# Chunk 1's first and last 16 rows stored partly by GpSimd's software queue (15 partitions) and partly by sync (113 partitions)

## The chip, the cores and the metric

The kernel runs on one core of a Trainium2 chip. The metric is the device time of one execution in microseconds (us). A run's time is given as the median of its executions; "span" is the length of the one execution that the profiler recorded, about 1.3 us shorter than its time. The data path matters most here: transfers between HBM (the chip's main memory) and SBUF (the core's 128-partition memory) run on 16 DMA engines, and the page of a profile counts the packets of all queues as shares of the same 16 (in the kernel before 97.5%, 0.6% and 0.4% for its three data queues). The traces do not number the engines; where this text speaks of one engine, its packets were chained, each starting within a few ns of where another ended.

## The reference

```python
x_flat = x.reshape(-1, 256)             # 32768 rows of 256 float32, 33.5 MB
y = x_flat @ W                          # W is 256 x 256
lora_out = ((x_flat @ lora_A) * lora_E) @ lora_B
return (y + scale * lora_out).reshape(16, 2048, 256)   # float32, 33.5 MB
```

The kernel folds the low-rank part into `W` first and then does one product per row. It reads 33.5 MB and writes 33.5 MB.

## The kernel before

The rows are cut into 4 chunks. In a chunk each of the 128 partitions holds 64 neighbouring rows (64 KB) in a buffer, a "home"; results are written over the inputs and stored from there. Sync issues nearly all transfers, in a fixed order: `L` is a load, `S` a store, followed by chunk, first row and last row.

```python
ORDER = [
    ("A",),
    # ... loads of chunks 0, 1 and of rows 0 to 16 of chunk 2 ...
    ("L", 2, 16, 64),
    ("S", 0, 0, 40),
    ("S", 0, 40, 64),
    ("L", 3, 0, 32),      # these two wait for the stores of chunk 0: three homes, four chunks
    ("L", 3, 32, 64),
    ("S", 1, 2, 64),
    ("S", 2, 0, 64),
    ("S", 3, 0, 64),
]
SHARED = (1, 0, 2)            # rows 0 and 1 of chunk 1 are stored apart:
SHARES = ((0, 5), (5, 126))   # partitions 0-4 and 5-125 by GpSimd, 126-127 by sync
HELD = (2, 16)                # where GpSimd issues them and then waits for ("S", 0, 0, 40)
# ...
            else:                                     # a store, in the sync program
                if c == SHARED[0]:
                    sync.wait_ge(s_shared, 1)
                    share(sync, SHARES[-1][1], P, stored_rest)
                sync.wait_ge(s_done, ends.index((c * ROWS + e) // CG - 1) + 1)
                sync.dma_start(out=y_chunks[c, :, s:e, :], in_=at_home).then_inc(...)
# ...
            if (c, b) == HELD:                        # in the GpSimd program
                gpsimd.wait_ge(s_shared, 1)
                for s, e in SHARES:
                    share(gpsimd, s, e, shared_stored)
                for op in HOLDERS:
                    gpsimd.wait_ge(stored[op], 16)
```

The odd split of two rows is there for its side effect: in the trace of the kernel before the 121-partition software store did not load all 16 DMA engines alike: 15 took four 4,096-byte packets each and one a single packet of 2,052 bytes, so one engine is spared 14 KB.

## Time and profile before

| | before |
|---|---|
| median of the first 3 runs | 162.38 us (161.68 to 162.63) |
| span of the profiled run | 160.4 us |
| moved | 67.43 MB, mean 420 GB/s |
| last store issued | 117.8 us |
| last packets of the 16 DMA engines end | 158.4 to 159.9 us, mean 158.9 |

From the page of the kernel before, the span, the busiest compute engine, and the DMA rows (40 slices of the span; DMA is the busy share of the 16 engines in tenths, where 9 is 90% or more):

```profile
span 160.4 us, 2030 instructions
PE 93.2 (58%) x782; PEld 82.0 (51%) x782; DVE 45.4 (28%) x66; ACT 66.1 (41%) x65; POOL 67.9 (42%) x72
DMA  7999999999899997989999999979998998998992
GB/s 259 444 409 460 441 415 482 425 400 466 376 523 454 405 392 317 482 351 421 472 411 460 417 409 482 511 333 459 491 433 360 507 441 360 507 425 376 507 425 114
q1 hardware_dynamic: 2308, 66.87, 97.5%
q0 software_dynamic: 112, 0.26, 0.4%
```

The DMA engines are full throughout and no compute engine is above 58%. The last two lines give a queue's packets, MB and share of the engines' time: the software queue (q0, GpSimd) carries 0.26 of 67 MB.

The timeline of sync's queue in the kernel before (start, duration, operation, count), its later part:

```profile
75.60 7.74 SPq L153 DMA_DIRECT2D home<-in_x_dram  x2
83.38 0.34 SPq L166 DMA_DIRECT2D out_dram<-home  x1
83.77 34.37 SPq L161 DMA_DIRECT2D out_dram<-home  x3
```

The last load is issued at 83 us, the store of chunk 1 at 83.8 us, and the last store at 117.8 us. From there to the end, 42 us, the queue only drains, so a compute engine or an issue that comes a few us later costs nothing.

The same kernel by stretches of the span (from:to, length, busy time and count of the engines, then TensorE's granted clock, the DMA share and GB/s):

```profile
core 0: us, PE busy (x) PEld busy (x) DVE busy (x) ACT busy (x) POOL busy (x), PEclk, DMA share, GB/s
66.00:74.00 8.00, 0.00 (x0) 0.00 (x0) 0.00 (x0) 0.00 (x0) 0.00 (x0) 0.50 1.00 432
74.00:82.00 8.00, 5.18 (x32) 4.52 (x33) 1.59 (x3) 1.65 (x2) 4.28 (x5) 0.61 1.08 463
100.00:106.00 6.00, 6.00 (x57) 5.56 (x56) 3.39 (x5) 4.76 (x5) 4.75 (x5) 1.00 1.12 480
106.00:118.00 12.00, 10.70 (x98) 9.70 (x96) 4.91 (x8) 9.11 (x9) 5.65 (x6) 1.00 1.03 444
118.00:150.00 32.00, 0.00 (x0) 0.00 (x0) 0.00 (x0) 0.00 (x0) 0.00 (x0) 0.55 1.00 434
```

The last two columns are the ones to read together. The share lies about 1 (its scatter of a tenth comes from packets at the edges of a stretch), and with it go about 434 GB/s. A 65,536-byte packet takes 2.418 us, 27.1 GB/s, and 16 engines at that rate make 434. So in this trace full engines go with full speed.

### The profile page before, as it was taken

What the parts mean: (1) busy time and instruction counts of PE and PEld (TensorE: products, weight loads), DVE (VectorE), ACT (ScalarE), POOL (GpSimd) and SP (SyncE); (2) the same over time, 40 slices, a digit from 0 to 9 for tenths busy, and PEclk for the clock granted to TensorE, in tenths of its full rate; (3) what the DMA queues carried; (4) which work ended last, traced back from release to release, by engine and by line L of the source; (5) the groups of instructions that cost most, each with busy time, mean ns of one, the idle gap of its engine ahead of it and who ended that gap; (6) DMA issues with size and microseconds to landing.
All of it is one profiled execution on the core that took longest, in us unless ns stands there. A gap on an engine that the chain in (4) does not pass through costs nothing.

```text
span 160.4 us, 2030 instructions
## 1 busy us (share of the span) xinstructions
PE 93.2 (58%) x782; PEld 82.0 (51%) x782; DVE 45.4 (28%) x66; ACT 66.1 (41%) x65; POOL 67.9 (42%) x72
## 2 busy tenths in 40 slices
PE   2979969959999990000899999999910000000000
PEld 1359958959999990000799999999900000000000
DVE  0155534525555550000155555555400000000000
ACT  3016774747777772000167777777720000000000
POOL 1527838377777731101677777777100000000000
PEclk9999999999999998555599999999996555555555
DMA  7999999999899997989999999979998998998992
GB/s 259 444 409 460 441 415 482 425 400 466 376 523 454 405 392 317 482 351 421 472 411 460 417 409 482 511 333 459 491 433 360 507 441 360 507 425 376 507 425 114
DMA packets 2631, 67.43 MB, mean 420 GB/s; under 512 B 496, under 2 KB 512, under 8 KB 708
## 3 DMA queue, kind: packets, MB, share of 16 engines
q1 hardware_dynamic: 2308, 66.87, 97.5%
q10 hardware_dynamic: 208, 0.28, 0.6%
q0 software_dynamic: 112, 0.26, 0.4%
q14 instruction: 3, 0.02, 0.0%
HBM read 33.85 MB, written 33.55 MB: 420 GB/s over the span
## 4 chain that ended last, share of the span: by engine, by line
DMA 43%; PE 26%; POOL 1%; ACT 1%; SPq 1%; issue 0%; ACTq 0%
DMA out_dram<-home 30%; PE psum_y L255 17%; DMA home<-in_x_dram 13%; PE psum_xt L244 9%; POOL stage L193 1%; ACT home L209 1%; SPq L153 0%; ACTq L213 0%; SPq L326 0%; SPq L290 0%
## 5 line engine op out<-in xcount | busy, mean ns | idle before, releaser
L209 ACT COPY home<-psum_y 128x1024 f32<-128x1024 f32 x64 | 64.8, 1012 | 49.6 <-PE psum_y L255 49.6
L193 POOL CAST stage<-home 128x1024 bf16<-128x1024 f32 x64 | 66.0, 1040 | 37.3 <-PE psum_xt L244 13.4
L255 PE MATMUL psum_y<-weff,xt 128*128 128x256 bf16 x512 | 67.3, 275 | 0.0
L228 DVE COPY xt<-psum_xt 128x1024 bf16<-128x1024 bf16 x64 | 44.3, 692 | 62.0 <-PE psum_xt L244 62.0
L255 PEld LDWEIGHTS psum_y<-weff,xt 128*128 128x128 bf16 x512 | 50.6, 99 | 5.5
L244 PE MATMUL psum_xt<-ident,stage 128*128 128x128 f32 x260 | 40.8, 281 | 20.6 <-POOL stage L193 20.1
L244 PEld LDWEIGHTS psum_xt<-ident,stage 128*128 128x128 f32 x260 | 31.2, 144 | 23.4 <-issue 22.1
L268 PE MATMUL psum_y<-ident 128*128 128x512 f32 x4 | 3.8, 1098 | 2.9 <-POOL ident L171 2.9
L166 POOL DMA_DIRECT2D out_dram<-home x2 | 1.2, 596 | 5.7 <-DMA home<-in_x_dram 5.7
L268 PEld LDWEIGHTS psum_y<-ident 128*128 128x128 f32 x4 | 1.2, 323 | 3.9 <-POOL ident L171 2.9
L218 DVE TENSOR_SCALAR ate<-psum_y,e_sb 16x256 f32<-16x256 f32 x1 | 0.5, 471 | 7.2 <-PE psum_y L271 7.2
L209 ACT ACT_TABLE_LOAD x1 | 1.3, 1283 | 2.0 <-SPq L290 2.0
L277 PE MATMUL psum_y<-b_sb,ate 16*128 16x256 f32 x4 | 1.3, 447 | 0.0
L277 PEld LDWEIGHTS psum_y<-b_sb,ate 16*128 16x128 f32 x4 | 0.8, 242 | 0.4 <-issue 0.3
L169 POOL MEMSET ident<- 128x128 f32 x1 | 0.2, 205 | 1.7 <-SPq L290 1.7
L271 PEld LDWEIGHTS psum_y<-ident,a_sb 128*16 128x16 f32 x2 | 0.3, 133 | 1.2 <-issue 1.2
L232 DVE TENSOR_TENSOR weff<-w_sb,psum_y 128x512 bf16<-128x512 f32 x1 | 0.7, 686 | 0.6 <-PE psum_y L277 0.6
L271 PE MATMUL psum_y<-ident,a_sb 128*16 128x128 f32 x2 | 0.6, 418 | 0.0
L171 POOL TENSOR_SCALAR_AFFINE_SELECT ident<-ident 128x128 f32<-128x128 f32 x1 | 0.3, 287 | 0.2 <-POOL ident L169 0.2
L312 POOL MEMSET const-float32-0.0<- 128x1 f32 x1 | 0.1, 98 | 0.2 <-issue 0.2
L312 POOL MEMSET const-bfloat16-1.0<- 128x1 bf16 x1 | 0.1, 101 | 0.0
L312 POOL MEMSET const-uint8-127<- 128x1 uint8 x1 | 0.1, 101 | 0.0
(1 smaller groups left out, 0.1 us busy)
## 6 DMA issues: line engine op xcount, KB each, us to landing
home<-in_x_dram SPq DMA_DIRECT2D x4, 4096.0 KB, 24.4
out_dram<-home SPq DMA_DIRECT2D x1, 7936.0 KB
home<-in_x_dram SPq DMA_DIRECT2D x3, 2048.0 KB, 13.2
home<-in_x_dram SPq DMA_DIRECT2D x1, 6144.0 KB, 58.2
out_dram<-home SPq DMA_DIRECT2D x1, 5120.0 KB, 48.7
home<-in_x_dram SPq DMA_DIRECT2D x1, 3072.0 KB, 20.0
out_dram<-home SPq DMA_DIRECT2D x1, 3072.0 KB, 46.4
home<-in_x_dram SPq DMA_DIRECT2D x1, 1024.0 KB, 5.5
```

The lines of the kernel that those rows point to most:

```text
L166: engine.dma_start(out=y_chunks[c, first:last, s:e, :], in_=home(c)[first:last, s:e, :]).then_inc(landed, 16)
L193: gpsimd.tensor_copy(out=stage[g % NS][:], in_=home(c)[:, b:b + CG, :]).then_inc(s_stage[g % UNROLL], 1)
L209: scalar.copy(out=home(c)[:, b:b + CG, :], in_=psum_y[g % NY][:]).then_inc(s_free[(g + NY) % UNROLL], 1)
L218: vector.tensor_scalar(out=ate[:], in0=psum_y[0][:R, :KT, :P], scalar1=e_sb[:], scalar2=float(scale), op0=ALU.mult, op1=ALU.mult,).then_in ...
L228: vector.tensor_copy(out=xt[g % NX][:], in_=psum_xt[g % NT][:].bitcast(BF16)).then_inc(s_xt[g % UNROLL], 1)
L232: vector.tensor_add(out=weff[:], in0=w_sb[:], in1=psum_y[1][:, :KT, :]).then_inc(s_free[0], 1)
L244: ins = tensor.transpose(psum_xt[i % NT][:, b, :], words[:, b, :], ident[:])
L255: ins = tensor.matmul(psum_y[i % NY][:, b, :], xt[i % NX][:, b, t::KT], weff[:, t, :], start=(t == 0), stop=(t == KT - 1),)
L268: tensor.matmul(psum_y[1][:, :2, :], ident[:], ident[:, None, :].to_broadcast([P, 4, P]), start=True, stop=True)
L271: ins = tensor.transpose(psum_y[0][:R, t, :P], a_sb[:, t, :], ident[:])
L277: ins = tensor.matmul(psum_y[1][:, t, :], ate[:, t, :], b_sb[:], start=True, stop=True)
L312: nc = _bacc.Bacc("TRN2", target_bir_lowering=False, num_devices=1)
```

## The change

Its intent is to spare one DMA engine more work than before: 32 KB in place of 14. Two tiny stores around the large software store are meant to choose the engine. The diff, cut to its core:

```diff
-    ("S", 1, 2, 64),
+    ("S", 1, 16, 48),
-SHARED = (1, 0, 2)
-SHARES = ((0, 5), (5, 126))
+SHARED = 1
+END_ROWS = 16
 # sync
-                if c == SHARED[0]:
+                if c == SHARED:
                     sync.wait_ge(s_shared, 1)
-                    share(sync, SHARES[-1][1], P, stored_rest)
+                    share(sync, end_rows(slice(16, P)), stored_rest)
+                    for q in (0, 3):
+                        share(sync, lambda rows: in_pieces(rows)[:1, q, :, :], stored_rest)
+                    sync.wait_ge(shared_stored, 3 * 16)
 # ...
+    def in_pieces(rows):
+        return rows[:].rearrange("p (q b) k -> p q b k", b=END_ROWS)
+    def end_rows(p):
+        return lambda rows: in_pieces(rows)[p, ::3, :, :]          # rows 0-15 and 48-63
+    def middles(p):
+        return lambda rows: in_pieces(rows)[p, 1:3, 0, :64]        # tiny, stored again later
 # GpSimd, at HELD
-                for s, e in SHARES:
-                    share(gpsimd, s, e, shared_stored)
+                for part in (middles(slice(0, 5)), end_rows(slice(1, 16)), middles(slice(5, 17))):
+                    share(gpsimd, part, shared_stored)
```

So the end rows, 32 KB per partition and 4 MB in all, now go as 112 partitions by sync, partition 0 by sync, and partitions 1 to 15 by GpSimd. The wait on `shared_stored` keeps the tiny stores from racing with the store of the middle rows.

More of the change, by code (lines that the diff above doesn't have):

```diff
@@ L103 @@
     stored_rest = nc.alloc_semaphore("stored_rest")
-    n_rest = 1 + sum(op[0] == "S" and op not in waited for op in ORDER)
+    n_rest = 3 + sum(op[0] == "S" and op not in waited for op in ORDER)
     ends = sorted((c * ROWS + e) // CG - 1 for kind, c, s, e in (op for op in ORDER if op[0] == "S"))
@@ L156, in sync_program, with share @@
             else:
-                if c == SHARED[0]:
+                if c == SHARED:
                     sync.wait_ge(s_shared, 1)
-                    share(sync, SHARES[-1][1], P, stored_rest)
+                    share(sync, end_rows(slice(16, P)), stored_rest)
+                    for q in (0, 3):
+                        share(sync, lambda rows: in_pieces(rows)[:1, q, :, :], stored_rest)
+                    sync.wait_ge(shared_stored, 3 * 16)
                 sync.wait_ge(s_done, ends.index((c * ROWS + e) // CG - 1) + 1)
                 sync.dma_start(out=y_chunks[c, :, s:e, :], in_=at_home).then_inc(stored.get(op, stored_rest), 16)
-        sync.wait_ge(shared_stored, 16 * len(SHARES))
-    def share(engine, first, last, landed):
-        c, s, e = SHARED
-        engine.dma_start(out=y_chunks[c, first:last, s:e, :], in_=home(c)[first:last, s:e, :]).then_inc(landed, 16)
+    def in_pieces(rows):
[4 more added lines that the diff above has]
+        return lambda rows: in_pieces(rows)[p, 1:3, 0, :64]
+    def share(engine, part, landed):
+        engine.dma_start(out=part(y_chunks[SHARED]), in_=part(home(SHARED))).then_inc(landed, 16)
     def gpsimd_program():
@@ L209, in scalar_program @@
             scalar.copy(out=home(c)[:, b:b + CG, :], in_=psum_y[g % NY][:]).then_inc(s_free[(g + NY) % UNROLL], 1)
-            if (c, b) == SHARED[:2]:
+            if (c, b + CG) == (SHARED, ROWS):
                 scalar.drain().then_inc(s_shared, 1)
```

## The prediction

> **What bounds the kernel now.** The DMA engines. The page gives 67.43 MB in a span of 160.4 us (420 GB/s); its DMA row stands at 7 to 9 tenths in nearly every slice, PE is 58% busy, POOL 42%, ACT 41%. The chain of waits ends with the last ScalarE copy at 116.73 us; the last store is issued at 117.8 us and 42 us of queued stores follow. So no compute wait moves the end. In the packet records a 65,536-byte packet takes 2.418 us (27.1 GB/s, 434 for 16 engines); 67.43 MB at that rate are 155.5 us. What is left to win is unevenness among the 16 engines.
>
> **How uneven.** I chained the packets of the trace, each starting where another ended, into 16 engines. Their last packets end from 158.42 to 159.89 us, mean 158.9. Perfect levelling is worth 1.0 us, 0.6%. The three last end at 159.37, 159.57 and 159.89. The one at 159.37 was some 1.2 us behind at 62 us, and is the one that the 121-partition software store already spares: 15 engines took four 4,096-byte packets each, this one a single 2,052-byte packet, 14 KB (0.5 us) less.[...] The other two were late for other causes: one shared with an 8,192-byte instruction fetch at 86.6 us (0.3 us gap and a packet 0.5 us long), one had eight 63,488-byte packets 0.15 us long each.
>
> **What the change does.** Chunk 1's end pieces (32 KB per partition) go as 112 partitions, 7 per engine, by sync (16,384-byte packets, 611 ns elsewhere in the trace), one partition spread over all, and 15 by the software queue, one per engine, so that one engine gets 32 KB less: 1.2 us instead of 0.5 us.[...] If it is the slow one, it ends near 158.8 us; all others get about 2 KB (0.07 us) more. The two other late engines then set the end: gain 0 to 0.4 us, perhaps 0.5 on average where runs spare differently.
>
> **Costs.** One more software store, about 0.6 us of GpSimd, inside a hold that already idles 10.8 us for a store of chunk 0. Sync now waits for the software stores (landed 7.7 and 12.5 us after issue before; I estimate 12 to 20 us, as more packets each wait behind a hardware packet of 1.5 us) before the middle of chunk 1: until 76 to 84 us. Before, that store was issued at 83.8 us with about 16 us of loads still queued. Both are off the path.
>
> **Prediction.** 161.9 us, range 161.0 to 163.3. Chances: faster 0.01, same 0.97, slower 0.02.
>
> **What would show it.** The DMA row stays full to the end; the 15-partition store has data on 15 engines; the spared engine is no longer among the last three; the sync wait leaves no hole.
>
> **What would make it wrong.** Another engine spared than the slow one: the slow one then ends about 0.5 us later. Or [...]16,384-byte packets take longer than 611 ns: 1 to 3 us slower.

Three passages that no trace or run of this case shows are cut from it, and marked: a comparison for the 121-partition store, how the tiny stores were to choose the engine and why each execution should then spare the same one, and how 16,384-byte packets might come to take longer. 161.9 us is the 162.38 us of the first three runs less about 0.5, the upper end of the gain named. That one partition would be spread over all engines no trace had shown; it is a forecast, and the result below contradicts it. The 1 to 3 us of the last sentence stand without a derivation, as the author's estimate.

## The result, and the profile after

| | before | after |
|---|---|---|
| median | 162.03 us (161.68 to 162.63, 4 runs) | 169.03 us (167.83 to 170.64, 4 runs) |
| span of the profiled run | 160.4 us | 167.7 us |
| last packets end | 158.4 to 159.9, mean 158.9 | 160.4 to 167.4, mean 163.3 |
| last store issued | 117.8 us | 122.5 us |

The ratio is 1.0403 (95% interval 1.0332 to 1.0474): slower, far outside the predicted range of 161.0 to 163.3. A ratio here is the mean time of one kernel's fast runs over that of the other's fast runs of the same rounds, so not quite the ratio of the medians. One of the four runs of after (170.64) counts as slow and is not in the ratio; the profiled one is fast.

The page of the changed kernel, the same lines as above:

```profile
span 167.7 us, 2033 instructions
PE 93.1 (56%) x782; PEld 81.8 (49%) x782; DVE 45.4 (27%) x66; ACT 66.1 (39%) x65; POOL 68.6 (41%) x73
DMA  7999999999999899998999999999999999999960
GB/s 274 406 434 459 404 469 453 414 430 403 418 547 399 375 344 469 389 285 365 422 426 424 430 430 352 385 395 391 465 430 485 438 406 422 485 406 422 438 281 16
q1 hardware_dynamic: 2548, 66.63, 94.5%
q0 software_dynamic: 112, 0.50, 1.8%
```

The DMA row is as full as before and the bytes are the same within 0.02 MB, yet the span is 7.3 us longer. The software queue moves twice its former bytes and takes 1.8% of the engines' time in place of 0.4%. The last two GB/s figures (281 and 16) are a tail in which few engines still work.

Sync's queue in the changed kernel:

```profile
79.74 7.51 SPq L153 DMA_DIRECT2D home<-in_x_dram  x2
87.30 1.10 SPq L176 DMA_DIRECT2D out_dram<-home  x3
88.51 34.30 SPq L164 DMA_DIRECT2D out_dram<-home  x3
```

The loads of chunk 3 are issued 4.1 us later, because they wait for the stores of chunk 0, which landed later. Otherwise the order and the pace are as before: between the end rows at 87.3 us and the middle at 88.5 us there is no long wait, so the new wait for the software stores costs nothing here.

The stretches of the changed kernel:

```profile
66.00:74.00 8.00, 0.00 (x0) 0.00 (x0) 0.00 (x0) 0.00 (x0) 0.00 (x0) 0.50 1.05 382
74.00:82.00 8.00, 1.04 (x5) 1.00 (x6) 0.00 (x0) 0.00 (x0) 2.02 (x2) 0.50 0.97 366
100.00:106.00 6.00, 6.00 (x57) 5.60 (x56) 3.04 (x5) 4.51 (x6) 4.81 (x5) 1.00 0.93 344
106.00:118.00 12.00, 12.00 (x112) 11.15 (x111) 6.31 (x10) 9.32 (x10) 9.37 (x9) 1.00 1.04 408
118.00:150.00 32.00, 3.37 (x31) 2.86 (x29) 1.30 (x2) 3.53 (x4) 0.00 (x0) 0.63 1.00 434
```

Here is the loss. The engines are busy (share 0.93 to 1.05), but at 66 to 82 us, when the software stores run, and at 100 to 118 us, when the end rows go out by sync, they move 344 to 408 GB/s. At 118 us all is well again. Busy engines with fewer bytes mean that single packets took longer.

The packet records show which. A 16,384-byte packet takes 611 ns elsewhere in these traces. Of the 30 such packets of the 15-partition software store 23 took more than 700 ns; their mean is 1,588 ns and the longest took 3,053 ns. Of the 226 that sync sent for the end rows the mean is 675 ns, with 26 over 700 ns. The losses fall unevenly: the spared engine is through first, at 160.4 us, and the last is 7 us behind it. On that last engine the final five packets of the end rows took 1.02 to 1.51 us each, 3.3 us together over 611 ns apiece.

### The profile page after: what moved, and what is told of

Same layout as the page of the kernel before. It is cut to its first block, busy times and chain, and to the rows that moved or that the text cites. A ratio compares the mean times of both kernels' runs of the same rounds, so it can differ in the third digit from the quotient of the medians.

```text
span 167.7 us, 2033 instructions
## 1 busy us (share of the span) xinstructions
PE 93.1 (56%) x782; PEld 81.8 (49%) x782; DVE 45.4 (27%) x66; ACT 66.1 (39%) x65; POOL 68.6 (41%) x73
## 4 chain that ended last, share of the span: by engine, by line
PE 38%; DMA 18%; another core or an unknown queue 12%; POOL 3%; issue 1%; SPq 1%; ACT 1%
PE psum_y L265 25%; DMA home<-in_x_dram 18%; PE psum_xt L254 13%; POOL stage L203 2%; POOL out_dram L176 1%; SPq L153 1%; ACT home L219 1%; SPq L336 0%; SPq L300 0%
## 5 line engine op out<-in xcount | busy, mean ns | idle before, releaser
L254 PE MATMUL psum_xt<-ident,stage 128*128 128x128 f32 x260 | 40.3, 278 | 25.3 <-POOL stage L203 24.9
L176 POOL DMA_DIRECT2D out_dram<-home x3 | 1.8, 601 | 4.9 <-DMA home<-in_x_dram 4.9
```

Of the source, the lines that this page charges most:

```text
L176: engine.dma_start(out=part(y_chunks[SHARED]), in_=part(home(SHARED))).then_inc(landed, 16)
L254: ins = tensor.transpose(psum_xt[i % NT][:, b, :], words[:, b, :], ident[:])
```

## The experiments

The theories, formed after this reading:

1. The partitions read at the same moment. Supposed: a store is slow when the engines read certain partitions at once, neighbours such as 1 to 15 above all. In the changed kernel 23 of the 30 packets of the 15 neighbours took over 700 ns, and 26 of the 226 packets of the 112 partitions, 7 to an engine. The runs below vary the partitions. Passages of the expectations that explain the loss by a grouping of the partitions, which no run shows, are cut and marked; the times expected under theory 1 stand as estimates.
2. The pieces: 16 KB at a pitch of 64 KB in HBM, two per partition, are slow.
3. The software queue, its large packets, or the wait for it.
4. Partition 0: both its pieces went to a single engine, which I had not expected: the trace has two 16,384-byte packets for it and none of 1,024. I took them for two packets of 1.21 and 1.51 us on the engine that ended last. That was a misreading, and the expectation of b_single_spread below rests on it: those two end the 112-partition store on their engine. Partition 0's are two packets of 611 ns on another engine, each between two four-byte packets that end a store.

### a_all_sync: all end rows by sync over 128 partitions

```diff
-                    share(sync, end_rows(slice(16, P)), stored_rest)
-                    for q in (0, 3): ...                  # partition 0
-                    sync.wait_ge(shared_stored, 3 * 16)
+                    share(sync, end_rows(slice(0, P)), stored_rest)
-                for part in (middles(...), end_rows(slice(1, 16)), middles(...)): ...   # GpSimd
```

> The end rows go in one store over all 128 partitions by sync; no software store, no wait for it. Theory 1 ([...]in the 15-partition software store and in the 112-partition store, plus two whole pieces of partition 0 on one engine): all of it is gone, 16,384-byte packets take 611 ns throughout, time 161.5 to 163. Theory 2 (the pieces themselves, 16 KB at a pitch of 64 KB in HBM, two per partition, are slow): the loss of the end rows stays, 164 to 168. Theory 3 (the software queue): 161.5 to 163, as theory 1.

Measured: 161.82 us (161.61 to 162.15), ratio 1.0009 (0.9989 to 1.0029). In its trace the 16,384-byte packets of the end rows have a mean of 614 ns. Theory 2 falls: the same pieces cost nothing when all 128 partitions go in one store. One stretch of it, for comparison with the runs below:

```profile
106.00:118.00 12.00, 11.23 (x103) 10.18 (x101) 5.45 (x8) 9.33 (x10) 6.20 (x6) 1.00 1.04 446
```

### b_single_spread: partition 0 shared among 16 engines

```diff
-                    for q in (0, 3):
-                        share(sync, lambda rows: in_pieces(rows)[:1, q, :, :], stored_rest)
+                    for q in (0, 3):
+                        for h in (0, 1):
+                            share(sync, lambda rows: in_pieces(rows)[:1, q, :, h * 128:h * 128 + 128], stored_rest)
```

> The changed kernel, with partition 0's two pieces cut into four stores of 16 runs of 512 bytes, so that 16 engines share them. In the changed kernel each of the two 16,384-byte pieces went to one engine, the one that ended last (1.21 and 1.51 us). Theory 1: that engine is relieved of 2.7 us and the last end falls from 167.4 to about 165.5 of the span; time 166.5 to 168. If the one-engine pieces were not on the critical engine in general: no change, 168.5 to 169.5.

Measured: 169.52 us (167.87 to 169.89), ratio 1.0445: no gain, so theory 4 falls as an explanation of the loss, and my expectation under theory 1 was wrong too. The pieces were spread (64 packets of 512 bytes), and yet the last engines ended at 167.8 and 168.2 us of the span. It is not one engine's two extra packets that make the tail, since engines are just as late without them. On the last engine of this trace the final five of its 14 packets of the 112-partition store took 1.27 to 1.52 us, 3.7 us together over 611 ns apiece.

### c_no_software: 112 and 16 partitions, both by sync

```diff
-                    for q in (0, 3): ...                  # partition 0
-                    sync.wait_ge(shared_stored, 3 * 16)
+                    share(sync, end_rows(slice(0, 16)), stored_rest)
-                for part in (middles(...), end_rows(slice(1, 16)), middles(...)): ...   # GpSimd
```

> The changed kernel with partitions 0 to 15 stored by sync in one 16-partition store, beside the 112-partition one: the same pieces, no software queue, no wait for it, nothing on one engine alone. Theory 1: [...]their packets take 1.2 to 3 us in place of 0.61, time 165 to 168. Theory 3 (software queue or its wait): 161.5 to 163.

Measured: 167.43 us (167.34 to 167.80), ratio 1.0348. No software queue, no wait for it, and still 5.6 us over a_all_sync, which stores the same bytes in pieces of the same size. Theory 3 is not needed for most of the loss. The stretches show it moved: 66 to 74 us is whole again, and the loss is where the end rows now all go.

```profile
66.00:74.00 8.00, 0.00 (x0) 0.00 (x0) 0.00 (x0) 0.00 (x0) 0.00 (x0) 0.50 1.03 446
106.00:118.00 12.00, 9.94 (x92) 8.97 (x89) 4.78 (x7) 8.62 (x9) 5.18 (x5) 1.00 1.03 298
```

The longest of its 16,384-byte packets took 4,780 ns.

### d_soft_only and e_soft_apart: 15 neighbouring partitions against 15 spread ones

Both are a_all_sync with the three software stores added as an extra ahead of it. They differ in one slice.

```diff
 # d_soft_only, against the changed kernel
-                    share(sync, end_rows(slice(16, P)), stored_rest)
-                    for q in (0, 3): ...                  # partition 0
                     sync.wait_ge(shared_stored, 3 * 16)
+                    share(sync, end_rows(slice(0, P)), stored_rest)
 # e_soft_apart, against d_soft_only
-... end_rows(slice(1, 16)) ...
+... end_rows(slice(0, 127, 9)) ...
```

> All end rows by sync over 128 partitions as in a_all_sync, and ahead of them, as an extra, the three software stores of the change (15 neighbouring partitions, 1 to 15) with the wait for them; the 480 KB are written twice, 30 KB or 1.1 us per engine. Theory 1[...] their 16,384-byte packets take 1.2 to 3 us as in the changed kernel, time 164.3 to 167. Software queue or its wait: the same. No cost but the bytes: 162.7 to 163.3.

> As d_soft_only, but the 15 partitions are every ninth (0, 9, ... 126)[...]; same queue, bytes, packets and wait. Theory 1: the software packets take about 611 ns[...], the loss of d_soft_only goes but for the bytes: 162.5 to 163.5. Software queue or its wait: as d_soft_only, 164.3 to 167.

Measured: d_soft_only 167.29 us (167.16 to 167.38), ratio 1.0328; e_soft_apart 164.09 us (162.64 to 164.91), ratio 1.0126 (1.0035 to 1.0217). Same queue, bytes, packets and wait; only the choice of partitions differs, and it is worth 3.2 us. The four runs of e_soft_apart scatter by 2.3 us (its verdict against the kernel before is "unclear"), but the slowest of them is 2.2 us under the fastest of d_soft_only. This is the sharpest test. First the stretches of d_soft_only, then those of e_soft_apart:

```profile
66.00:74.00 8.00, 0.00 (x0) 0.00 (x0) 0.00 (x0) 0.00 (x0) 0.00 (x0) 0.50 1.08 386
74.00:82.00 8.00, 1.06 (x5) 1.00 (x6) 0.00 (x0) 0.00 (x0) 2.02 (x2) 0.50 0.96 371
```

```profile
66.00:74.00 8.00, 0.00 (x0) 0.00 (x0) 0.00 (x0) 0.00 (x0) 0.00 (x0) 0.50 1.08 465
74.00:82.00 8.00, 4.72 (x30) 4.14 (x31) 1.38 (x2) 1.44 (x2) 4.10 (x4) 0.61 0.95 395
```

With the partitions apart the first stretch is at full rate. In the second stretch e_soft_apart is still below it, at a share of 0.95. The packets, counted in the traces:

```
16,384-byte packets       software store, 30 packets     end rows by sync
                          mean ns   over 700 ns          count  mean ns  over 700 ns
changed kernel              1588        23                 226      675       26
c_no_software                  -         -                 256      854       49
d_soft_only                 1565        24                 256      613        1
e_soft_apart                 632         1                 256      613        0
a_all_sync                     -         -                 256      614        1
f_halves                       -         -                 256     1074      185
```

The choice of partitions also changes where the pieces go in HBM: 64 KB apart for neighbours, 576 KB for every ninth. No run separates the partitions from the places in HBM. But the software store's own packets were not the only slow ones: while the 15 neighbours' packets ran, sync's 40,960-byte packets, which store chunk 0 to other addresses, were slowed too, up to 3,687 ns in place of 1,514: in each of three traces (the changed kernel, b, d) five such packets over 1,650 ns, on four engines. e_soft_apart has none over 1,602 ns. By what means the neighbours hinder one another is not shown.

e_soft_apart is slower than expected (162.5 to 163.5). The 30 KB per engine written twice are 1.1 us at 27.1 GB/s, an estimate; the rest over a_all_sync, 2.3 less 1.1, about 1.2 us, is not the software packets, whose mean is 632 ns. Part of it sits in sync's 24,576- and 32,768-byte packets after 62 us: together they ran 0.9 us per engine over their plain 912 and 1,213 ns, against 0.2 us in a_all_sync. Why they did is not shown.

### f_halves: the end rows in two stores of 64 partitions

```diff
-                    share(sync, end_rows(slice(0, P)), stored_rest)
+                    share(sync, end_rows(slice(0, 64)), stored_rest)
+                    share(sync, end_rows(slice(64, P)), stored_rest)
```

> The end rows as in a_all_sync, in two stores by sync over partitions 0 to 63 and 64 to 127; no software store. Theory 1: [...]packets of 611 ns take about 1.2 us and 4 MB take 19 us in place of 9.7: time 169 to 172. If [...]only small stores suffer: 161.5 to 162.5.

Measured: 169.70 us (169.43 to 169.72), ratio 1.0472. The median 16,384-byte packet took 1,267 ns, twice 611. From its stretches:

```profile
106.00:118.00 12.00, 10.30 (x95) 9.30 (x93) 4.84 (x7) 8.97 (x9) 5.25 (x6) 1.00 1.00 224
118.00:150.00 32.00, 0.00 (x0) 0.00 (x0) 0.00 (x0) 0.00 (x0) 0.00 (x0) 0.55 1.02 439
```

All engines are busy (share 1.00) at half the bytes, 224 GB/s, where a_all_sync moved 446 in the same stretch. No software queue is in this kernel, so the loss is found with sync's stores alone as well.

### i_extra_112 and j_extra_128: the 112-partition store by itself

Both add an extra store of 3.5 MB ahead of everything else of chunk 1, and store all end rows once more, over 128 partitions, before the last chunk's store.

```diff
 # i_extra_112, against a_all_sync
-                    share(sync, end_rows(slice(0, P)), stored_rest)
+                    share(sync, end_rows(slice(16, P)), shared_stored)
+                if c == 3:
+                    sync.wait_ge(shared_stored, 16)
+                    share(sync, end_rows(slice(0, P)), stored_rest)
 # j_extra_128, against i_extra_112
-                    share(sync, end_rows(slice(16, P)), shared_stored)
+                    share(sync, lambda rows: in_pieces(rows)[:, ::3, :14, :], shared_stored)
```

> To time the 112-partition store by itself: all_sync's stores, with the change's 112-partition store of the end rows added ahead as an extra (224 KB or 8.3 us per engine at the rate of before); the end rows are stored once more, by 128 partitions, between the stores of chunks 2 and 3. Theory 1: [...]171.5 to 173.5, that is 1.5 to 3.5 us over j_extra_128. If 7 partitions per engine cost nothing: as j_extra_128, about 170.1.

> The control of i_extra_112: an extra store of as many bytes, 14 of the 16 end rows at each end over all 128 partitions. [...]161.8 and 8.3 for the bytes, 169.8 to 170.4, packets of 14,336 bytes at their plain rate.

Measured: i_extra_112 172.01 us (171.95 to 172.19), j_extra_128 170.46 us (169.83 to 170.90), of the same rounds. The difference, 1.55 us (1.05 to 2.36 between single runs), is what 112 partitions, 7 per engine, cost over 128 for 3.5 MB, at the low edge of what I expected. The stretches of i_extra_112 and then j_extra_128:

```profile
106.00:118.00 12.00, 9.86 (x91) 8.90 (x88) 4.69 (x7) 8.52 (x9) 5.08 (x5) 1.00 1.04 416
```

```profile
106.00:118.00 12.00, 11.35 (x104) 10.29 (x102) 5.54 (x8) 9.32 (x10) 6.25 (x6) 1.00 1.05 452
```

### g_no_share, g_no_share_5 and h_four_rows: what sparing an engine is worth

```diff
 # g_no_share, against the kernel before
-    ("S", 1, 2, 64),
+    ("S", 1, 0, 64),          # and all software stores, and sync's share, removed
 # h_four_rows, against the kernel before
-SHARED = (1, 0, 2)
+SHARED = (1, 0, 4)            # and ("S", 1, 4, 64)
```

> The kernel before without its software store: chunk 1 goes in one store by sync. It measures what sparing one engine 14 KB was worth. From the trace of before: the spared engine would end about 0.5 us later, at 159.9, as late as the last one now: 0 to 0.8 us slower than before, 162 to 163.

> The kernel before with 4 rows of chunk 1 in the software store in place of 2: one engine is spared 28 KB in place of 14 KB, 1.0 in place of 0.5 us. g_no_share (no sparing) was as fast as before, so whichever engine is spared is not the one that ends last: 161.4 to 162.2, no gain.

> The same kernel as g_no_share, in five rounds, as the candidate that beats both kernels: no software store at all. First time: ratio 0.9986, interval 0.997 to 1.0003. Expected 0.997 to 1.001: at least as fast as before; a gain above 0.3% is not expected.

Measured: g_no_share 161.57 us, ratio 0.9986 (0.9970 to 1.0003); again in five rounds 161.76 us, ratio 0.9989 (0.9968 to 1.0010). h_four_rows 162.79 us, ratio 1.0078 (0.9993 to 1.0163). With no engine spared at all the kernel is as fast as before. Sparing twice as much does not help and may cost a little. So the goal that the change pursues was worth nothing here, which I missed: I had read an engine's lateness in one trace and expected relief to show at the end.

g_no_share is the simplest of all and not slower than any; its gain over the kernel before is not clear of zero, so I call it equal.

## Why the prediction was wrong, point by point

- **The DMA engines bind, and no compute wait moves the end: right.** In the changed kernel the last store is issued at 122.5 us, 45 us before the end. GpSimd's hold grew from 10.8 to 15.0 us without harm, though I had put its growth at 0.6 us.
- **"15 by the software queue, one per engine, so that one engine gets 32 KB less: 1.2 us instead of 0.5 us": this is the step that failed.** I costed the spared engine's gain and gave the other 15 engines the plain 611 ns per packet. Measured: 1,588 ns in the mean; with neighbours in d_soft_only 1,565 ns, with every ninth partition in e_soft_apart 632. Those two runs put the choice of partitions at 3.2 us.
- **"16,384-byte packets take longer than 611 ns": named as what would make it wrong, at 1 to 3 us, but given almost no weight.** I named it for the 112-partition store. Measured alone: 1.55 us. I looked for the danger in the 112-partition store and not in the 15-partition one, which the paired runs put higher. In the changed kernel itself the tail on the last engine came in the 112-partition store (3.3 us in five packets).
- **"One partition spread over all": wrong.** Both pieces went to one engine, as two packets of 611 ns. Spreading them gained nothing measurable.
- **The tiny stores choose the spared engine: not shown.** In all four traces with these stores (the changed kernel, b, d and e) exactly one engine got none of the 15 partitions, and it was the one that had data of both the 5-partition and the 12-partition store. No run took the tiny stores away, and that each execution spares the same engine no run tested.
- **"If it is the slow one": it was not.** In the two traces of the 121-partition form (before, h_four_rows) the spared engine was the last of the 16 to begin the first store of chunk 0. In the four traces of the new form it was not: in the changed kernel it began at 61.43 us, ahead of most, while the latest began at 62.41. And g_no_share shows that sparing was worth nothing either way.
- **The software stores' landing (12 to 20 us) and the sync wait off the path: right.** The 15-partition store landed 14.4 us after its issue, the last tiny one 16.2 us. The hardware packet of 1.5 us is in both traces: 48 of the 66 software packets of before, and all 30 of the 15-partition store, began within 12 ns of the end of a 40,960-byte packet of sync's, whose median is 1,514 ns.
- **"What would show it": three of the four signs came true.** The 15-partition store had data on 15 engines, the spared engine was not among the last three, and the sync wait left no hole; only the full DMA row failed, in the last two slices. The three signs could not tell a gain from a loss of 7 us, since none of them looks at how long a packet takes.

Between the changed kernel (169.03) and a_all_sync (161.82) lie 7.2 us. The neighbouring partitions take 3.2 and the 112-partition store 1.55 by the paired runs. About 1.2 us belong to having the large software store at all (e_soft_apart, less its extra bytes), without a shown cause. That leaves some 1.3 us, if the parts simply add, which no run shows. The traces give another cut: the last packet ends 7.6 us later than in a_all_sync (167.4 against 159.8); 4.4 us of this is a later mean of the 16 engines (163.3 against 159.0), and 3.2 us is unevenness, as the last engine lies 4.0 us beyond the mean against 0.8. Why the slow packets of the 112-partition store pile up on one or two engines was not taken apart.

## What to carry to other kernels

A DMA engine that is busy need not be moving at its rate (in f_halves a share of 1.00 went with 224 GB/s, before with 434): read the busy share and the GB/s of the same stretch together, and when they part, look at the duration of packets of one size. Before splitting a store by partitions, write down which partitions the engines read at the same moment; here 15 neighbours cost 3.2 us more than 15 spread by nine, and in two halves the median packet took 1,267 ns, against a mean of 614 in one whole. And before sparing a late engine, remove the sparing that is already there: here nothing changed, and twice the sparing brought no gain either.

## What else the traces showed

- 15 neighbouring partitions beside a full store on another queue: their packets had a mean of 1,565 ns in d_soft_only, against 632 ns at a stride of nine, and with the neighbours the full store's own packets took up to 3,665 ns in place of 1,514.
- 112 partitions used all 16 engines and took 1.55 us longer for 3.5 MB than 128.
- A 16,384-byte run of one partition was not split in the changed kernel: one engine took it as one packet of 611 ns. In b_single_spread the run was cut into shorter ones (64 packets of 512 bytes) and was shared.
- The 121-partition store, one 2 KB run per partition, put data on 16 engines by 8 partitions (four 4,096-byte packets on 15 of them, one of 2,052 bytes on the last). The 15-partition store of the changed kernel, two runs per partition, put two 16,384-byte packets on each of 15 engines; the 5- and the 12-partition store, two runs per partition, took 5 and 12 engines, with a 512-byte packet per partition.
- In the trace of before one 8,192-byte instruction fetch at 86.6 us took 0.31 us, and the packet that starts where it ends took 1,747 ns in place of 1,213; that engine ended second last.
